# An RMSNorm and QKV projection with Strassen products: four instead of eleven row tiles transposed by TensorE, and a new order of the opening part

## The chip, the cores and the metric

The kernel runs on one core of a Trainium2 chip. A core has five engines that run side by side, each through its own queue in order: TensorE (PE in the profile; its weight loads are PEld), VectorE (DVE), ScalarE (ACT), GpSimd (POOL) and SyncE (SP), which here issues nearly all DMA transfers. Sixteen DMA engines, shared by all transfers, move data between HBM and the core's memory SBUF. TensorE writes only to PSUM, whose eight banks DVE and ACT read out. The metric is the time of one execution on the device in microseconds (us); lower is better.

## What is computed

```python
def reference(x, gamma, w_qkv, eps):      # x: 8 x 1024 x 768, w_qkv: 768 x 2304, float32
    rms = np.sqrt(np.mean(x ** 2, axis=-1, keepdims=True) + eps)
    x_norm = x / rms * gamma
    return np.matmul(x_norm, w_qkv).astype(np.float32)
```

The 8192 rows of x are normalised by their root mean square, scaled by gamma, and multiplied by the weights: an 8192 x 768 by 768 x 2304 product.

## The kernel before

**Tiles.** The rows make 64 tiles of 128. Tiles 0 to 3 are multiplied in bf16 in the plain way (`mm`, L519) while the weights arrive. The other sixty tiles make thirty pairs, 2 to 31, and each pair is multiplied by Strassen's scheme in Winograd's form: the pair's two tiles and the two halves of the 768 inputs give four blocks a11 to a22, the weights of one of three column chunks (768 columns each) give b11 to b22, and seven products of blocks take the place of eight. A product (`product`, L689) is three matmuls of 384 columns in f16.

**Weights.** Sixteen pieces are loaded (`load_w`, L445), multiplied by gamma and cast to bf16 into `w_b` (`conv`: DVE L451, ACT L453, POOL L455). For each chunk an upper bound of the weights is found (`bound` and what follows it) and the quarters are scaled to f16 (`quad`, L617 to L621), and four sums of them are made (`tsum`, L627).

**Rows.** For the first four tiles: `load_x` (L440), `cast` to bf16 and `cp` (both of them L459 on DVE, L461 on ACT), `stat` (L470 and L472: sum of squares and root, ACT), `tr` (transposes by TensorE, L483). For a tile of a pair: `load_x`, `pstat` (L637, ACT), `prms` (L641, ACT), `precip` (L646, DVE), `pcast` to f16 with the row's scale (L651, DVE). Then the tile must be turned so that the inputs lie along the partitions. There are two ways. `ptr` lets TensorE make six transposes into PSUM (L674), and `pcp` copies the result to SBUF (again L459 or L461). `pxbar` is one DMA transpose from SBUF to SBUF, issued by SP (L655). Four sums of the pair's blocks follow (`osum`, L669, DVE or POOL): s1 is read by product 5, s2 by 6, s3 by 7, s4 by 3.

**Results.** The products of a chunk gather in three PSUM banks, and are read out by `hold` (L696 DVE, L698 ACT), `join` (L714, DVE: bank times scale plus a held part) and `last` (L718, ACT). `evac` (L535, L537) does this for the first four tiles. `store` (L541) and `pstore` (L743) are issued by SP. From pair 4 on some results are kept in `w_b`, whose weights are no longer needed then, in areas handed out by `result` in a circle. The last product of all is cut in two (`end_piece`, L725).

**Order.** No scheduler arranges the work: every engine takes its instructions in the order in which the program issues them, and that order is written out. `PLAN` lists the steps of the opening part (everything up to and including pair 14) with a time in us that only sorts them. From pair 15 (`STEADY`) a loop sets the same pattern for each pair and chunk, in slots (0.4875 us, `SLOT`, one product) after `HEAD_END`. Steps of both are merged by their times. In the opening part the plan chooses, step by step, which engine does a conversion, a sum, a hold or a copy, and whether a tile is turned by `ptr` or by `pxbar`. In the regular part all tiles take `pxbar` and all sums are POOL's. Each pair of the loop is prepared ahead:

```python
when((-45, -57)[odd] + 4.5 * i, pcast, t)
when((-42, -54)[odd] + 4.5 * i, pxbar, t)
```

**The start.** PE first turns gamma (`gamma_in`, L552), then runs `idle` (L558), matmuls of zeros that nobody reads, 512 columns each, and then the transposes of the first tiles.

Of the kernel before, what the change touches and what calls it, by code (L numbers as in the profile page):

```python
# [15 lines left out]
HEAD_END = 169.75  # L16
# [3 lines left out]
    (0.000, "load_x", 1), (1.160, "load_x", 3), (4.040, "stat", 1), (4.041, "cast", 1, "DVE"), (4.042, "load_x", 2),  # L20
    (4.043, "gamma_in"), (4.044, "idle", 6, 512), (5.030, "cast", 3, "DVE"), (5.031, "load_w", 2), (5.260, "tr", 1),
    (5.820, "cp", 1, "DVE"), (5.821, "stat", 3), (6.820, "stat", 2), (6.821, "load_w", 3), (6.822, "load_x", 0),
    (6.823, "tr", 3), (6.824, "load_w", 4), (7.480, "conv", 2, 3, "POOL"), (7.481, "load_w", 1),
    (7.482, "cast", 2, "DVE"), (7.483, "tr", 2), (8.141, "conv", 3, 4, "ACT"), (8.142, "cp", 2, "DVE"),
    (8.320, "mm", 1, 0, "3"), (8.660, "mm", 2, 0, "3"), (8.921, "mm", 1, 0, "4"), (9.131, "stat", 0),
    (10.331, "cp", 3, "ACT"), (10.332, "mm", 2, 0, "4"), (10.333, "conv", 4, 5, "POOL"), (10.334, "cast", 0, "DVE"),
    (10.335, "tr", 0), (10.631, "mm", 2, 0, "5"), (10.847, "mm", 1, 0, "5"), (10.848, "load_w", 0),
    (10.849, "cp", 0, "DVE"), (11.062, "mm", 0, 0, "5"), (11.772, "conv", 0, 0, "ACT"),
    (11.773, "conv", 1, 2, "POOL"), (11.774, "mm", 0, 0, "4"), (11.775, "conv", 0, 1, "POOL"), (11.776, "recip", 1),
    (11.777, "mm", 1, 0, "2"), (11.778, "load_w", 6), (11.779, "recip", 2), (11.780, "mm", 0, 0, "2"),  # L30
    (13.092, "conv", 6, 3, "ACT"), (13.093, "conv", 6, 2, "POOL"), (13.094, "load_w", 7),
    (13.095, "mm", 3, 0, "012345"), (13.907, "mm", 2, 0, "012"), (13.908, "recip", 3), (13.909, "recip", 0),
    (13.910, "bound", 0, 1, "DVE"), (13.911, "load_w", 5), (14.107, "evac", 3, 0, "ACT"),
    (14.754, "evac", 2, 0, "ACT"), (14.755, "load_w", 9), (14.756, "load_w", 10), (14.757, "mm", 0, 0, "01"),
    (14.758, "bound", 0, 0, "DVE"), (14.759, "conv", 7, 4, "POOL"), (14.986, "mm", 1, 0, "01"),
    (14.987, "conv", 7, 5, "DVE"), (15.418, "mm", 1, 512, "23"), (15.849, "mm", 0, 512, "23"),
    (15.850, "conv", 5, 0, "DVE"), (16.281, "mm", 0, 512, "54"), (16.282, "conv", 5, 1, "ACT"),
    (16.514, "bound", 1, 0, "DVE"), (16.515, "bound", 0, 2, "ACT"), (16.713, "mm", 2, 512, "23"), (18.254, "fold", 0),
    (18.255, "mm", 1, 512, "01"), (18.256, "mm", 1, 512, "45"), (18.375, "conv", 10, 5, "ACT"), (18.376, "load_w", 8),
    (18.377, "mm", 3, 512, "45"), (18.378, "load_x", 4), (18.544, "bound_tr", 0), (18.664, "mm", 0, 512, "01"),  # L40
    (18.665, "load_x", 5), (19.015, "evac", 1, 512, "ACT"), (19.016, "load_w", 14), (19.017, "conv", 9, 3, "POOL"),
    (19.018, "load_w", 15), (19.019, "conv", 9, 2, "POOL"), (19.615, "evac", 0, 512, "ACT"), (19.616, "bound_top", 0),
    (19.617, "bound_all", 0), (19.618, "mm", 0, 0, "3"), (19.619, "conv", 10, 4, "POOL"),
    (19.695, "conv", 8, 1, "POOL"), (19.696, "scales", 0), (19.697, "mm", 3, 512, "23"),
    (20.375, "quad", 0, "b12", "POOL"), (20.376, "mm", 1, 1024, "23"), (21.645, "quad", 0, "b11", "POOL"),
    (21.646, "mm", 3, 512, "01"), (21.647, "mm", 2, 512, "01"), (21.648, "mm", 1, 1024, "45"),
    (21.649, "conv", 8, 0, "ACT"), (21.650, "pstat", 4), (21.825, "pstat", 5), (21.826, "bound", 1, 2, "DVE"),
    (21.827, "mm", 2, 1024, "45"), (22.150, "mm", 0, 1024, "01"), (22.581, "mm", 2, 512, "45"),
    (23.013, "mm", 1, 1024, "01"), (23.014, "conv", 14, 1, "ACT"), (23.225, "prms", 2),
    (23.226, "bound", 1, 1, "DVE"), (23.227, "evac", 3, 512, "DVE"), (23.228, "load_w", 12), (23.884, "fold", 1),  # L50
    (23.885, "evac", 0, 0, "ACT"), (24.034, "precip", 2), (24.035, "load_w", 13), (24.036, "mm", 2, 1024, "01"),
    (24.075, "conv", 14, 0, "ACT"), (24.076, "mm", 0, 1024, "45"), (24.308, "mm", 2, 1024, "23"),
    (24.309, "tsum", 0, "t1", "DVE"), (24.740, "bound_tr", 1), (24.741, "load_x", 7), (25.060, "bound_top", 1),
    (25.061, "mm", 0, 1024, "23"), (25.062, "conv", 14, 2, "ACT"), (25.063, "quad", 0, "b21", "POOL"),
    (25.291, "mm", 3, 1024, "45"), (25.292, "evac", 2, 512, "ACT"), (25.723, "bound_all", 1),
    (25.843, "mm", 1, 2048, "012"), (25.844, "pcast", 5), (26.171, "mm", 2, 2048, "012"),
    (26.172, "conv", 15, 4, "POOL"), (26.173, "load_x", 6), (26.498, "mm", 3, 1024, "23"),
    (26.499, "evac", 1, 1024, "ACT"), (26.500, "conv", 12, 3, "ACT"), (26.501, "load_x", 17),
    (26.502, "evac", 0, 1024, "DVE"), (26.503, "conv", 15, 5, "POOL"), (26.504, "conv", 12, 2, "POOL"),
    (26.505, "load_w", 11), (26.930, "mm", 3, 2048, "012"), (27.257, "ptr", 5), (27.617, "mm", 3, 1024, "01"),  # L60
    (27.618, "load_x", 9), (27.619, "conv", 15, 3, "POOL"), (27.620, "evac", 2, 1024, "DVE"),
    (27.621, "evac", 1, 0, "DVE"), (28.049, "mm", 3, 2048, "345"), (28.050, "quad", 0, "b22", "ACT"),
    (28.051, "pstat", 7), (28.052, "scales", 1), (28.377, "mm", 0, 2048, "345"), (28.378, "pcp", 5, "DVE"),
    (28.704, "mm", 1, 2048, "345"), (28.945, "evac", 3, 2048, "ACT"), (28.946, "conv", 13, 4, "POOL"),
    (29.475, "store", 3, 2, 2048, 256), (29.476, "conv", 13, 5, "POOL"), (29.477, "pstat", 6),
    (29.478, "mm", 0, 2048, "012"), (29.479, "bound", 2, 1, "DVE"), (30.305, "evac", 0, 2048, "ACT"),
    (30.306, "mm", 2, 2048, "345"), (30.307, "mm", 0, 1536, "45"), (30.695, "prms", 3),
# [295 lines left out]
CW = 384  # L363
# [8 lines left out]
def kernel(  # L372
# [14 lines left out]
    add = mybir.AluOpType.add  # L387
# [6 lines left out]
    Kw, N = w_qkv.shape  # L394
# [297 lines left out]
    def hold(p, c, bank, name, eng):  # L692
# [4 lines left out]
        else:  # L697
            nc.scalar.activation(out=o, in_=pb, func=AF.Copy, scale=SC[c], bias=0.0)  # L698

    spare = []  # L700

    def result(p, c, i, j):
        t = 2 * p + i
# [135 lines left out]
```

## Time and profile before

| what | value |
|---|---|
| median of three runs | 355.81 us (354.83 to 356.18) |
| the profiled execution, whole | 355.04 us |
| its span, first to last instruction | 353.0 us |
| DMA engines' share, 40 to 100 us | 1.03 to 1.07 |
| last weight piece landed | 32.0 us |
| first product of pair 15 | 176.2 us |
| last matmul ends | 349.0 us |

The profile page gives the busy time of each engine, its share of the span, and the number of instructions. The chain of waits starts at the last instruction and goes back, at each step, to what released it: time on that chain is what sets the end. A timeline lists the instructions of one engine in order, equal neighbours merged, with the idle time before each and what ended it. The busy time of PE adds overlapping instructions of a pipeline, so a mean duration there is longer than the time between two starts: product matmuls last 326 ns each and follow one another every 163 ns. The DMA share is packet time over the time of all sixteen engines; packets overlap, so it can pass 1.

### The profile page before, as it was taken

Reading aid. Unit: us, or ns where it says so; the run is one execution under the profiler, and the core shown is the slowest. Engines: PE = TensorE matmul, PEld = TensorE weight load, DVE = VectorE, ACT = ScalarE, POOL = GpSimd, SP = SyncE. Lnnn points to the kernel's source line nnn. Section 1 sums busy time; section 2 is a strip of 40 time slices with the busy share of each in tenths; the row PEclk is TensorE's granted clock in tenths of the full one; section 3 lists DMA queues with packets and bytes.
Section 4 is the critical chain, followed back from the end, with each engine's and each line's share of the span. In section 5 each row is a group of like instructions: output and inputs, shape, how many; then the busy total and the mean of one; then the engine's idle time right before and its main releaser. Section 6 shows DMA issues by size and latency. Waiting matters only on the chain.

```text
span 353.0 us, 6601 instructions
## 1 busy us (share of the span) xinstructions
PE 342.4 (97%) x2113; PEld 203.6 (58%) x2116; DVE 267.1 (76%) x503; ACT 242.6 (69%) x497; POOL 123.5 (35%) x137
## 2 busy tenths in 40 slices
PE   5899999999999999999999999999999999999995
PEld 3346566655666566556556566566566566666653
DVE  3789998988898787676877778676777867676663
ACT  6799898884766665767657576776757676665543
POOL 1496656421041304444354160614407061434000
PEclk9999999999999999999999999999999999999999
DMA  7999999999999899999999999999999999967565
GB/s 275 392 381 351 336 398 364 358 390 377 297 395 331 320 300 318 388 262 382 350 351 355 311 356 320 375 335 334 381 308 332 348 358 353 358 248 277 203 257 223
DMA packets 80637, 117.80 MB, mean 334 GB/s; under 512 B 43606, under 2 KB 45532, under 8 KB 80604
## 3 DMA queue, kind: packets, MB, share of 16 engines
q1 hardware_dynamic: 80448, 117.30, 98.9%
q8 instruction: 16, 0.26, 0.3%
q14 instruction: 17, 0.14, 0.1%
q10 hardware_dynamic: 156, 0.10, 0.1%
HBM read 32.25 MB, written 75.50 MB: 305 GB/s over the span
## 4 chain that ended last, share of the span: by engine, by line
PE 91%; DVE 3%; DMA 2%; SPq 1%; issue 1%; ACT 0%
PE pm L689 84%; PE pm L519 6%; DMA wq<-in_w_qkv_dram 2%; DVE wq L627 1%; PE pm L674 1%; DVE ot L714 1%; DVE xb L651 1%; SPq L445 1%; SPq L440 0%; DVE xT L459 0%; ACT w_b L453 0%; PE pm L725 0%; DVE w_b L714 0%; DVE su L669 0%; ACT pp L698 0%
## 5 line engine op out<-in xcount | busy, mean ns | idle before, releaser
L689 PE MATMUL pm<-wq,su 128*128 128x384 f16 x1080 | 205.6, 326 | 0.4 <-DVE ot L714 0.4
L698 ACT ACTIVATE pp<-pm,sc 128x384 f32<-128x384 f32 x204 | 113.9, 579 | 71.1 <-PE pm L689 70.0
L689 PE MATMUL pm<-wq,xT 128*128 128x384 f16 x807 | 160.9, 326 | 0.6 <-DVE ot L714 0.6
L689 PEld LDWEIGHTS <-su 128*128 128x128 f16 x1080 | 105.3, 98 | 70.4 <-issue 1.2
L714 DVE SCALAR_TENSOR_TENSOR ot<-pm,sc,pp 128x384 f32<-128x384 f32 x172 | 100.2, 612 | 27.0 <-PE pm L689 24.3
L689 PEld LDWEIGHTS <-xT 128*128 128x128 f16 x807 | 78.8, 98 | 52.8 <-issue 1.0
L669 POOL TENSOR_TENSOR su<-xT 128x384 f16<-128x384 f16 x50 | 46.1, 938 | 147.0 <-PE pm L689 71.0
L714 DVE SCALAR_TENSOR_TENSOR w_b<-pm,sc,pp 128x384 f32<-128x384 f32 x98 | 58.4, 615 | 23.6 <-PE pm L689 22.4
L696 DVE TENSOR_SCALAR pp<-pm,sc 128x384 f32<-128x384 f32 x66 | 40.3, 614 | 21.1 <-PE pm L689 20.8
L637 ACT ACTIVATE sq<-x_t 128x768 bf16<-128x768 f32 x60 | 50.2, 836 | 0.7 <-DMA x_t<-in_x_dram 0.4
L651 DVE TENSOR_SCALAR xb<-x_t,rstd 128x768 f16<-128x768 f32 x60 | 39.8, 665 | 0.4
L718 ACT ACTIVATE ot<-pm,sc 128x384 f32<-128x384 f32 x48 | 27.4, 576 | 12.2 <-PE pm L689 11.0
L669 POOL TENSOR_TENSOR su<-xT,su 128x384 f16<-128x384 f16 x28 | 26.2, 936 | 23.1 <-PE pm L689 14.7
L718 ACT ACTIVATE w_b<-pm,sc 128x384 f32<-128x384 f32 x41 | 23.5, 576 | 13.7 <-PE pm L689 13.5
L669 POOL TENSOR_TENSOR su<-su,xT 128x384 f16<-128x384 f16 x26 | 24.9, 958 | 14.3 <-PE pm L689 10.0
L519 PE MATMUL pm<-w_b,xT 128*128 128x512 bf16 (+1 forms) x117 | 25.2, 357 | 1.6 <-POOL w_b L455 0.9
L519 PEld LDWEIGHTS <-xT 128*128 128x128 bf16 x120 | 11.2, 98 | 11.7 <-issue 1.6
L455 POOL TENSOR_SCALAR w_b<-wq,g_sb 128x512 bf16<-128x512 f32 (+1 forms) x16 | 11.6, 731 | 12.6 <-DMA wq<-in_w_qkv_dram 12.6
L637 ACT ACTIVATION_READ_ACCUMULATOR sq<-x_t 128x1 f32 x60 | 11.5, 192 | 0.0
L576 DVE TENSOR_REDUCE bnd<-w_b 128x1 f32<-128x1536 bf16 x6 | 10.3, 1748 | 0.6 <-ACT w_b L453 0.3
L621 POOL TENSOR_SCALAR wq<-w_b,inv 128x1152 f16<-128x1152 bf16 x8 | 9.7, 1224 | 1.8 <-DVE inv L605 1.8
L453 ACT ACTIVATE w_b<-wq,g_sb 128x512 bf16<-128x512 f32 (+1 forms) x12 | 7.8, 666 | 3.3 <-DMA wq<-in_w_qkv_dram 3.1
(56 smaller groups left out, 101.0 us busy)
## 6 DMA issues: line engine op xcount, KB each, us to landing
out_dram<-ot SPq DMA_DIRECT2D x110, 384.0 KB, 4.3
out_dram<-w_b SPq DMA_DIRECT2D x68, 384.0 KB, 4.5
x_t<-in_x_dram SPq DMA_DIRECT2D x64, 384.0 KB, 5.3
wq<-in_w_qkv_dram SPq DMA_DIRECT2D x10, 512.0 KB, 9.3
out_dram<-ot SPq DMA_DIRECT2D x8, 512.0 KB, 6.2
wq<-in_w_qkv_dram SPq DMA_DIRECT2D x4, 256.0 KB, 5.8
xT<-xb SPq DMA_TRANSPOSE x49, 5.0
wq<-in_w_qkv_dram SPq DMA_DIRECT2D x2, 384.0 KB, 9.7
```

The costliest lines, as they stand in the source:

```text
L455: nc.gpsimd.tensor_scalar(out=o, in0=i, scalar1=g, scalar2=1.0, op0=mult, op1=mult)
L519: nc.tensor.matmul(out=PM[t, n0][:, :nl], lhsT=XT[t][:, ko, :], rhs=w_b[:, ko, n0:n0 + nl], start=(b == 1), stop=(b == KO))
L576: nc.vector.tensor_reduce(out=o, in_=v, axis=mybir.AxisListType.XY, op=amax, apply_absolute_value=True)
L621: nc.gpsimd.tensor_scalar(out=o, in0=quad_view(c, q), scalar1=INV[c], scalar2=1.0, op0=mult, op1=mult)
L637: nc.scalar.activation(out=sq, in_=X[t], func=AF.Square, accum_out=SS[p][:, t % 2:t % 2 + 1])
L651: nc.vector.tensor_scalar(out=XB[t], in0=X[t], scalar1=SS[t // 2][:, t % 2:t % 2 + 1], scalar2=None, op0=mult)
L669: (nc.vector if eng == "DVE" else nc.gpsimd).tensor_tensor(out=block(p, q), in0=block(p, x), in1=block(p, y), op=op)
L689: nc.tensor.matmul(out=PB[k][:, :CW], lhsT=block(p, a)[:, ko, :], rhs=WQ[c, b][:, ko, :], start=(first and ko == 0), stop=(ko == KO // 2 - ...
L696: nc.vector.tensor_scalar(out=o, in0=pb, scalar1=SC[c], scalar2=None, op0=mult)
L698: nc.scalar.activation(out=o, in_=pb, func=AF.Copy, scale=SC[c], bias=0.0)
L714: nc.vector.scalar_tensor_tensor(out=result(p, c, i, j), in0=PB[p, c, bank][:, :CW], scalar=SC[c], in1=PART[p, c, held], op0=mult, op1=add)
L718: nc.scalar.activation(out=result(p, c, 1, 0), in_=PB[p, c, "a"][:, :CW], func=AF.Copy, scale=SC[c], bias=0.0)
```

## The change

Seven tiles of the opening part, 6, 8, 11, 13, 15, 17 and 19, are turned by `pxbar` instead of `ptr` and `pcp`; tiles 4, 5, 7 and 9 stay with TensorE, and tile 7's copy goes to ACT, tile 9's to DVE. The whole `PLAN` is written anew: the same loads, products and stores in another order up to pair 14, and other engines for some steps (DVE makes ten conversions instead of two and 20 sums instead of 16; POOL 13 conversions instead of 16 and 32 sums instead of 36; ACT seven conversions instead of twelve and 88 holds instead of 85). At the start tile x0 comes before x3 and weight piece 4 before the others, ACT casts tile 1 and copies tiles 0, 1, 2, and there are 14 fillers instead of six. `HEAD_END` is 3.5 smaller. In the loop the casts and DMA transposes of a pair come 2.8 to 3.8 slots later and 4.1 instead of 4.5 slots apart, and the sums half a slot later; s3 is now made last. The areas of `w_b` for results are taken from a list to which each goes back when its whole store is issued.

```diff
@@ -13,348 +13,345 @@
           6, 1024, 512), (0, 2, 1536, 512), (2, 4, 1536, 512), (4, 6, 1536, 512), (0, 3, 2048,
           256), (3, 6, 2048, 256)]
 
-HEAD_END = 169.75
+HEAD_END = 166.25
 STEADY = 15
 
 PLAN = [
-    (0.000, "load_x", 1), (1.160, "load_x", 3), (4.040, "stat", 1), (4.041, "cast", 1, "DVE"), (4.042, "load_x", 2),
-    (4.043, "gamma_in"), (4.044, "idle", 6, 512), (5.030, "cast", 3, "DVE"), (5.031, "load_w", 2), (5.260, "tr", 1),
-    (5.820, "cp", 1, "DVE"), (5.821, "stat", 3), (6.820, "stat", 2), (6.821, "load_w", 3), (6.822, "load_x", 0),
-    (6.823, "tr", 3), (6.824, "load_w", 4), (7.480, "conv", 2, 3, "POOL"), (7.481, "load_w", 1),
-    (7.482, "cast", 2, "DVE"), (7.483, "tr", 2), (8.141, "conv", 3, 4, "ACT"), (8.142, "cp", 2, "DVE"),
-    (8.320, "mm", 1, 0, "3"), (8.660, "mm", 2, 0, "3"), (8.921, "mm", 1, 0, "4"), (9.131, "stat", 0),
-    (10.331, "cp", 3, "ACT"), (10.332, "mm", 2, 0, "4"), (10.333, "conv", 4, 5, "POOL"), (10.334, "cast", 0, "DVE"),
-    (10.335, "tr", 0), (10.631, "mm", 2, 0, "5"), (10.847, "mm", 1, 0, "5"), (10.848, "load_w", 0),
-    (10.849, "cp", 0, "DVE"), (11.062, "mm", 0, 0, "5"), (11.772, "conv", 0, 0, "ACT"),
-    (11.773, "conv", 1, 2, "POOL"), (11.774, "mm", 0, 0, "4"), (11.775, "conv", 0, 1, "POOL"), (11.776, "recip", 1),
-    (11.777, "mm", 1, 0, "2"), (11.778, "load_w", 6), (11.779, "recip", 2), (11.780, "mm", 0, 0, "2"),
...
-    (32.278, "pcast", 6), (32.725, "quad", 1, "b21", "DVE"), (32.726, "store", 1, 0, 0, 1024),
...
-    (33.500, "product", 2, 0, 5), (33.988, "ptr", 6), (33.989, "pcp", 4, "DVE"), (34.348, "mm", 3, 1536, "01"),
...
-    (36.185, "osum", 2, "s4", "POOL"), (36.186, "mm", 0, 1536, "01"), (36.745, "pcp", 6, "DVE"),
...
-    (50.501, "product", 3, 2, 1), (51.465, "hold", 3, 2, "a", "p1", "ACT"), (51.965, "prms", 5), (51.966, "ptr", 8),
-    (51.967, "tsum", 2, "t1", "DVE"), (51.968, "tsum", 2, "t2", "POOL"), (51.969, "pcast", 9),
...
+    (0.000, "load_x", 1), (1.160, "load_x", 0), (1.580, "load_x", 2), (5.030, "cast", 0, "DVE"), (5.031, "load_w", 4),
+    (5.032, "load_w", 1), (6.820, "cast", 2, "DVE"), (6.821, "cast", 1, "ACT"), (6.822, "stat", 0),
+    (6.823, "load_w", 2), (6.824, "load_w", 3), (6.825, "gamma_in"), (6.826, "idle", 14, 512), (6.827, "tr", 1),
+    (7.480, "conv", 4, 5, "DVE"), (7.481, "tr", 0), (7.482, "cp", 0, "ACT"), (7.483, "tr", 2),
+    (7.484, "cp", 1, "ACT"), (8.050, "mm", 0, 0, "5"), (8.141, "conv", 1, 2, "DVE"), (8.266, "mm", 1, 0, "5"),
+    (8.267, "load_x", 3), (8.801, "conv", 2, 3, "DVE"), (8.802, "cp", 2, "ACT"), (8.803, "mm", 0, 0, "2"),
+    (8.926, "mm", 1, 0, "2"), (9.142, "mm", 2, 0, "5"), (9.371, "mm", 2, 0, "3"), (9.372, "stat", 1),
+    (9.461, "conv", 3, 4, "DVE"), (9.587, "mm", 0, 0, "3"), (9.803, "mm", 1, 0, "3"), (10.031, "mm", 0, 0, "4"),
+    (10.032, "recip", 0), (10.451, "stat", 3), (10.452, "load_w", 0), (11.772, "conv", 0, 1, "POOL"),
+    (11.773, "mm", 2, 0, "4"), (11.774, "conv", 0, 0, "ACT"), (11.775, "cast", 3, "DVE"), (11.776, "mm", 1, 0, "4"),
+    (11.777, "tr", 3), (12.612, "mm", 1, 0, "01"), (13.043, "mm", 0, 0, "01"), (13.044, "load_w", 6),
+    (13.045, "load_w", 7), (13.046, "stat", 2), (13.047, "load_w", 5), (13.092, "conv", 6, 2, "POOL"),
...
+    (32.575, "prms", 3), (32.576, "product", 2, 0, 1), (32.978, "evac", 2, 1024, "DVE"), (32.979, "product", 2, 0, 2),
+    (33.033, "mm", 2, 1536, "45"), (33.034, "hold", 2, 0, "a", "p1", "ACT"), (33.638, "precip", 3),
+    (33.639, "store", 0, 2, 2048, 256), (33.738, "join", 2, 0, 0, 0, "b", "p1"), (34.288, "pcast", 6),
+    (34.289, "load_x", 17), (34.290, "load_x", 16), (34.291, "load_x", 11), (34.998, "osum", 2, "s2", "DVE"),
+    (34.999, "mm", 0, 1536, "23"), (35.000, "mm", 1, 1536, "01"), (35.001, "mm", 2, 1536, "01"),
+    (35.002, "bound", 2, 2, "ACT"), (35.003, "mm", 0, 1536, "01"), (35.191, "mm", 1, 1536, "23"),
+    (35.192, "bound", 2, 0, "ACT"), (35.193, "quad", 1, "b22", "POOL"), (35.623, "product", 2, 0, 5),
+    (35.624, "tsum", 0, "t2", "DVE"), (36.110, "mm", 0, 1536, "45"), (36.111, "pcast", 7),
+    (36.568, "osum", 2, "s4", "DVE"), (36.569, "product", 2, 1, 1), (36.570, "pxbar", 6),
...
+    (47.425, "product", 2, 1, 4), (47.913, "product", 3, 0, 3), (47.914, "store", 2, 0, 0, 1024),
+    (47.915, "store", 0, 0, 0, 1024), (47.916, "join", 3, 1, 1, 1, "a", "p5"), (47.917, "pcast", 8),
+    (47.918, "pstore", 2, 0, 1), (48.478, "pxbar", 8), (49.728, "load_x", 13), (49.729, "product", 3, 1, 4),
...
@@ -654,7 +651,7 @@
         XT[t] = xTp.tile([P, KO, P], f16, name="xT")
         nc.sync.dma_start_transpose(out=XT[t], in_=XB[t])
 
-    SUMS = {"s1": ("a21", "a22", add), "s3": ("a11", "a21", sub), "s2": ("s1", "a11", sub), "s4": ("a12", "s2", sub)}
+    SUMS = {"s1": ("a21", "a22", add), "s2": ("s1", "a11", sub), "s4": ("a12", "s2", sub), "s3": ("a11", "a21", sub)}
 
     def block(p, q):
         if q[0] == "s":
@@ -697,14 +694,14 @@
         else:
             nc.scalar.activation(out=o, in_=pb, func=AF.Copy, scale=SC[c], bias=0.0)
 
-    spare = []
+    spare = [2 * CW * i for i in range(KO * N // (4 * CW))]
+    lent = {}
 
     def result(p, c, i, j):
         t = 2 * p + i
         if (t, "s", c) not in OUT:
             if p >= 4 and (c == 2 or (c == 1 and i == 1 and p % 2 == 0)):
-                s = 2 * CW * (len(spare) % (KO * N // (4 * CW)))
-                spare.append((t, c))
+                s = lent[t, c] = spare.pop(0)
                 OUT[t, "s", c] = w_b.rearrange("p k n -> p (k n)").bitcast(f32)[:, s:s + 2 * CW]
             else:
                 OUT[t, "s", c] = outp.tile([P, 1024], f32, name="ot")
@@ -741,6 +738,8 @@
         j0, j1 = (half[0], half[0] + 1) if half else (0, 2)
         n0 = 2 * CW * c
         nc.sync.dma_start(out=of[t * P:(t + 1) * P, n0 + CW * j0:n0 + CW * j1], in_=OUT[t, "s", c][:, CW * j0:CW * j1])
+        if (t, c) in lent and not half:
+            spare.append(lent.pop((t, c)))
 
 
     N_CH = N // (2 * CW)
@@ -766,12 +765,12 @@
                     t = 2 * p + i
                     when((-96, -103)[odd] + 7 * i, load_x, t)
                     when((-64, -71)[odd] + 7 * i, pstat, t)
-                    when((-45, -57)[odd] + 4.5 * i, pcast, t)
-                    when((-42, -54)[odd] + 4.5 * i, pxbar, t)
+                    when((-41.2, -53.8)[odd] + 4.1 * i, pcast, t)
+                    when((-38.2, -50.8)[odd] + 4.1 * i, pxbar, t)
                 when((-54.5, -61.5)[odd], prms, p)
-                when((-46, -58)[odd], precip, p)
+                when((-42, -54.6)[odd], precip, p)
                 for i, q in enumerate(SUMS):
-                    when(-7 + 0.01 * i, osum, p, q, "POOL")
+                    when(-6.5 + 0.01 * i, osum, p, q, "POOL")
             end = p == MT // 2 - 1 and c == N_CH - 1
             for i, u in ((1, 0), (5, 1), (2, 7.5 if end else 2), (6, 4), (3, 5), (7, 7 if end else 10), (4, 13)):
                 if not (end and i == 4):
```

## The prediction

> **What bounds the kernel now.** I read the page's first two parts, then the PE timeline, the chain of waits, and the timelines of ACT and DVE at the start.
>
> ```profile
> span 353.0 us, 6601 instructions
> ...
> PE 342.4 (97%) x2113; PEld 203.6 (58%) x2116; DVE 267.1 (76%) x503; ACT 242.6 (69%) x497; POOL 123.5 (35%) x137
> ...
> PE 91%; DVE 3%; DMA 2%; SPq 1%; issue 1%; ACT 0%
> ...
> 179.74 167.88 PE pm L689 x1032
> ```
>
> PE is the bound: from 179.74 us to 347.62 us the chain is 1032 product matmuls with no gap, 0.163 us each. The regular part can therefore gain nothing unless PE gets less work; what can change lies before 180 us. Pricing every PE instruction at its pace there (product 3 x 0.163 = 0.488; 512-column matmul 0.216; six f16 transposes 0.34), the work that waits after the first weight block is 333.1 us. That block's matmuls start at 12.89 and the last matmul ends at 349.0, so 3.0 us are lost to waits in between: about 0.6 up to 26 us, 0.1 at 33, 0.7 at 42 to 44, 0.4 at 58 to 73, 0.3 at 155, 0.6 at 180, 0.4 before the end pieces (3.1 with rounding). The other 4.0 us of the span are the last eviction and store, which stay.
>
> ```profile
> 2.77 2.74 PE L558 MATMUL pm<-const-float32-0.0 128*128 128x512 bf16 x6
> 5.31 1.49 PE L483 MATMUL pm<-ident,xb 128*128 128x128 bf16 x12
> 7.27 0.82 PE L483 MATMUL pm<-ident,xb 128*128 128x128 bf16 x6 [0.48 <-DVE xb L459]
> ...
> 10.89 1.46 PE L519 MATMUL pm<-w_b,xT 128*128 128x512 bf16 x6 [0.36 <-POOL w_b L455]
> 12.89 5.99 PE L519 MATMUL pm<-w_b,xT 128*128 128x512 bf16 x26 [0.54 <-ACT w_b L453]
> ```
>
> Columns: start, length, instruction; in brackets the idle time before it and its releaser. The six fillers take 0.43 us each and the first transposes 0.12; later 512-column matmuls take 0.216 and transposes 0.056. The array thus runs at half pace until about 8 us. At 12.89 PE waits for `conv 0,0`, ACT's conversion of the first weight block (DMA landing at 12.09, then 0.73 us).
>
> **Seven tiles leave TensorE.** The plan's transposes by TensorE go from eleven tiles to four (4, 5, 7, 9); tiles 6, 8, 11, 13, 15, 17, 19 take the DMA. PE loses 7 x 6 transposes.
>
> ```profile
> 51.69 0.34 PE pm L674 x6
> ...
> L674 PE MATMUL pm<-ident_h,xb 128*128 128x128 f16 x66 | 5.5, 219 | 0.0
> ...
> L459 DVE COPY xT<-pm 128x768 f16<-128x768 f16 x8 | 4.3, 550 | 0.4 <-PE pm L674 0.3
> ```
>
> The six stand in the chain of waits with 0.34 us (the 219 ns of the group overlap), so PE gains 7 x 0.34 = **-2.4 us**. With them go, net, five DVE copies of 0.55 us and two ACT copies of 0.80 us. DVE also gives up a bound (1.75), three holds (0.61 each), a cast and two copies of the first tiles (0.56 each), and takes eight conversions (0.49 each at full width), four sums (0.35) and an eviction (0.74): some 2 us less before the regular part, in a stretch where it is 88 to 92% busy (40 to 80 us).
>
> What is added is seven DMA transposes, each on SP and on the 16 DMA engines.
>
> ```profile
> xT<-xb SPq DMA_TRANSPOSE x49, 5.0
> ...
> DMA packets 80637, 117.80 MB, mean 334 GB/s; under 512 B 43606, under 2 KB 45532, under 8 KB 80604
> ```
>
> On SP one takes a median of 1.57 us to issue against 0.33 to 0.4 for a plain one, so 11 us more of SP; its issues fill 34 of the 64 us from 36 to 100, so there is room, though stores and loads behind each transpose go 1.5 us later. The DMA engines are the tight place: from 40 to 100 us their share is 1.03 to 1.07. The trace's DMA records show 768 packets of 256 B per transpose, 27 ns on average and 18 at best. That is 768 x 27 / 16 = 1.28 us of all engines, 9.0 us for seven; at 18 ns, 6.0. Loads and stores at their unqueued 122 ns per 3 KB packet leave only 2.4 us idle in those 60 us. Here a rule speaks against the change: the Trainium skill, "DMA: Bandwidth & Descriptors", under Latency and other measured facts, gives a DMA transpose an effective 261 GB/s, hence 0.75 us per 192 KB tile and 5.3 us for seven; its Specifications ask for 512 B and more per transfer for full rate, twice these packets. By the row 6.6 us would find no room, by the rule 2.9; either exceeds the idle time. But full DMA engines are not yet a late PE: PE already ran gapless from 78.20 to 154.60 beside a share of 1.07, except for one transpose of 0.34 us, since stores have buffers. What must arrive in time is the transpose. From issue to landing it takes 2.8 to 6.2 us, median 5.0; the new plan leaves 4 us for tile 8 (transpose at 48.5, first product at 52.5 in its times) and 5 to 6 for tiles 11, 12 and 13. I take 0 for this at PE, with 0 to +3.6 for the range and more for the rival below.
>
> **The start.** The new plan loads x tiles 1, 0, 2 and weights 4, 1, 2, 3 before x tile 3, gives most first conversions to DVE (0.49 us against 0.69 on POOL and 0.72 on ACT), and puts 14 fillers instead of 6 ahead of the transposes. PE takes them in order. From 2.77 us, at 0.43 us each until the pace doubles, and 0.216 after. By the row, half pace to 8.0, 12.2 fillers are done by then and the last at 8.4. The skill's rule ("TensorE: Matmul & The Clock Gate", Part 1) lets the clock rise after one busy window of about 3.4 us, which runs freely against the kernel: between 6.1 and past 8.8, so the fillers end between 7.5 and 8.75, which makes the sum of this part +0.6 to +1.9 where the row gives +1.5. I keep the row's 8.4.
>
> From there the chain runs over ACT, which now copies tiles 0, 1, 2. Two tiles' transposes 0.7 and hand-over 0.15 put the first copy at 9.25; three copies at 0.75 end at 11.5; then `stat 1` and `stat 3`, which the plan sets ahead of `conv 0,0`, cost 1.17 us each (4.00 to 5.17 in ACT's timeline): 13.84; `conv 0,0` at 0.72 ends at 14.56. PE, which has done eleven matmuls before it instead of ten, runs out at about 13.3 and waits. So the dense run starts at **14.6 instead of 12.89: +1.7**, less one matmul of 0.2 done early, **+1.5**. Bounds: a clock at 6.1 us gives 13.7 (+0.6); were the fillers hidden altogether, the block's landing would decide, as now (-0.2); all cold gives 14.95 (+1.9). Behind ACT stand `stat 2`, a bound, and evictions, all later by the same, and the PSUM banks they free.
>
> **The waits behind.** PE is 1.5 us later against DVE and the loads at 15 to 45 us, and DVE has less to do. The wait at 42 is DVE's: the chain stands on DVE from 36.13 to 42.34. I count the waits at 33 and 42 to 44 (0.8) and 0.3 of those at 58 to 73 as hidden: **-1.1**, between 0 (all come back behind the later ACT) and -2.0 (those at 73, 155 and 180 mostly go too).
>
> **At nothing.** The regular part's casts move by 2.8 to 3.8 slots, its sums by half a slot, and s3 goes last, as product 7 (its only reader) is. In the window from 180 us on, 26 casts take 610 to 621 ns and the sums 903 to 922, so they don't hinder one another now; and PE is gapless. If that cover went, a cast ahead of a join would cost PE up to the 0.6 us seen at 180, once. The list of borrowed output areas in `w_b` frees an area when its store is issued instead of taking them in a circle: a join could wait for a store of 4.5 us, hidden by the rest of the list.
>
> **Sum.** -2.4 + 1.5 - 1.1 = **-2.0 us**: span 351.0, that execution 353.0 instead of 355.04. The median before stands 0.77 above it, so I forecast **353.8**.
>
> **Rivals.**
> (1) *The start costs nothing*: the fillers end early or the ACT chain is shorter, and the dense run begins at 12.9. Then -1.7 more: **352.1**. For it: the block lands at 12.1 all the same. Against: ACT's strict order. 24%.
> (2) *The start costs in full and the later waits come back*, as ACT carries its lateness along: -2.4 + 1.5 = -0.9, **354.9**. For it: ACT is 94 to 99% busy from 20 to 40 us, so it doesn't catch up. 16%.
> (3) *The transposes land late*: between 36 and 100 us the DMA engines get 6.0 to 9.0 us more and have 2.4 to spare, and PE waits for the sums of pairs 3 to 9 by the remainder, 3.6 to 6.6 us: 357.4 to 360.4, at the middle **358.9**. It outweighs the gain from 2.0 us on, and shows as slower from 3.8, about 0.55 us for each of the seven tiles. For it: landing takes 5.0 us in the median where the plan leaves 4 to 6. Against: stores can be put off. 10%.
>
> The forecast keeps 50%; its own range is 352.7 to 355.0. A change of 0.5% is 1.8 us, about what a measurement of this kernel can tell from none: faster means under 354.0. Of the forecast's 50, 36 lie there; with rival 1 that is 60. Rival 2, the forecast's other 14 and 2 of rival 3 make 32 within; 8 are left for slower. For 8 in 10 I go from rival 1 less half a microsecond to the forecast plus half of what the returning waits and the cheaper transposes cost together ((1.1 + 3.6) / 2): 351.6 to 356.2.
>
> **What would show it.** Right: 24 transposes under L674; fillers ending near 8.4; `conv 0,0` on ACT ending near 14.5 and PE idle about 1.2 us before it; no DVE wait of PE at 42; the regular part still at 0.163 us. Wrong: PE or the sums waiting for DMA xT<-xb between 40 and 100 us (rival 3), or the dense run starting by 13 (rival 1).

## The result and the profile after

The changed kernel takes **353.52 us** in the median (353.44 to 353.78, four executions) against 355.81 before: a ratio of 0.9941, 95% interval 0.9921 to 0.9962. The forecast was 353.8. The gain is in the medians more than in the two profiled executions: the one of before was 0.77 us below its median and the one of the changed kernel 0.26 above, so whole executions went from 355.04 to 353.78 and spans from 353.0 to 352.0.

The page of the changed kernel, and the last long piece of its chain of waits:

```profile
span 352.0 us, 6558 instructions
...
PE 341.8 (97%) x2079; PEld 201.4 (57%) x2082; DVE 265.3 (75%) x504; ACT 242.1 (69%) x497; POOL 118.0 (34%) x130
...
PE 92%; ACT 4%; DVE 1%; issue 1%; DMA 1%; DVEq 0%; ACTq 0%
...
xT<-xb SPq DMA_TRANSPOSE x56, 5.0
```

```profile
198.63 18.70 PE pm L686 x114
...
219.69 126.96 PE pm L686 x780
```

(Line numbers are three lower than before: the product is L686.) PE is still the bound at 0.163 us a matmul, but the chain is whole only from 219.69 us; before it was whole from 179.74. The start, in PE's timeline:

```profile
2.99 5.65 PE L555 MATMUL pm<-const-float32-0.0 128*128 128x512 bf16 x14
8.48 1.17 PE L480 MATMUL pm<-ident,xb 128*128 128x128 bf16 x18
10.20 0.39 PE L516 MATMUL pm<-w_b,xT 128*128 128x512 bf16 x1 [0.56 <-ACT xT L458]
10.90 2.39 PE L516 MATMUL pm<-w_b,xT 128*128 128x512 bf16 x10 [0.31 <-ACT xT L458]
13.12 0.50 PE L480 MATMUL pm<-ident,xb 128*128 128x128 bf16 x6
14.52 1.67 PE L516 MATMUL pm<-w_b,xT 128*128 128x512 bf16 x6 [0.90 <-ACT w_b L450]
```

The fillers end near 8.5 and the dense run starts at 14.52, behind ACT's `conv 0,0`. ACT's timeline shows why:

```profile
9.35 2.20 ACT L458 COPY xT<-pm 128x768 bf16<-128x768 bf16 x3 [3.23 <-PE pm L480]
11.42 0.87 ACT L467 ACTIVATE sq<-x_t 128x768 bf16<-128x768 f32 x1
...
13.77 0.70 ACT L450 ACTIVATE w_b<-wq,g_sb 128x512 bf16<-128x512 f32 x1
```

Three copies, two `stat` and the conversion, end to end. Behind the start PE loses 2.8 us in all (its timeline against the price of its instructions, as before): 0.5 at 42, 0.1 at 55, 0.4 each at 155 and 199, 0.6 at 220, 0.4 before the end pieces, the rest in small pieces. The one at 42 is new in kind. First before, then the changed kernel's PE, and what its weight loads waited for between 38 and 44 us (us in all, times, longest):

```profile
42.38 0.22 PE L588 MATMUL pm<-ident,bmax 128*1 128x128 bf16 x1 [0.45 <-DVE ot L714]
```

```profile
41.85 1.15 PE L686 MATMUL pm<-wq,xT 128*128 128x384 f16 x6 [0.37 <-ACT pp L695]
```

```profile
PEld L686 <- DMA xT<-xb: 0.8, 1, 0.8
```

Product 3,1,1 reads tile 6, whose DMA transpose landed at 41.81. The timeline names ACT, but the weight load of the same product names the transpose, and PE starts 0.04 us after it landed.

### The profile page after: what moved, and what is told of

Its sections match the earlier page's. It is cut to its first block, busy times and chain, and to the rows that moved or that the text cites. A ratio compares the mean times of both kernels' runs of the same rounds, so it can differ in the third digit from the quotient of the medians.

```text
span 352.0 us, 6558 instructions
## 1 busy us (share of the span) xinstructions
PE 341.8 (97%) x2079; PEld 201.4 (57%) x2082; DVE 265.3 (75%) x504; ACT 242.1 (69%) x497; POOL 118.0 (34%) x130
## 4 chain that ended last, share of the span: by engine, by line
PE 92%; ACT 4%; DVE 1%; issue 1%; DMA 1%; DVEq 0%; ACTq 0%
PE pm L686 85%; PE pm L516 5%; PE pm L555 2%; ACT sq L576 1%; ACT xT L458 1%; DVE ot L711 1%; DMA g<-in_gamma_dram 1%; ACT ot L534 0%; ACT sq L467 0%; ACT pp L695 0%; PE pm L671 0%; DVE xb L648 0%; ACT w_b L450 0%; PE pm L480 0%; DVE pp L693 0%
## 5 line engine op out<-in xcount | busy, mean ns | idle before, releaser
L686 PE MATMUL pm<-wq,su 128*128 128x384 f16 x1080 | 203.8, 326 | 0.3 <-DVE pp L693 0.3
L695 ACT ACTIVATE pp<-pm,sc 128x384 f32<-128x384 f32 x207 | 116.5, 581 | 75.0 <-PE pm L686 72.7
L686 PE MATMUL pm<-wq,xT 128*128 128x384 f16 x807 | 159.3, 326 | 1.0 <-DVE ot L711 0.6
L686 PEld LDWEIGHTS <-su 128*128 128x128 f16 x1080 | 105.5, 98 | 70.1 <-issue 0.5
L686 PEld LDWEIGHTS <-xT 128*128 128x128 f16 x807 | 78.7, 98 | 54.1 <-issue 1.1
L666 POOL TENSOR_TENSOR su<-xT 128x384 f16<-128x384 f16 x52 | 49.6, 956 | 154.3 <-DMA xT<-xb 82.5
L693 DVE TENSOR_SCALAR pp<-pm,sc 128x384 f32<-128x384 f32 x63 | 38.4, 614 | 19.1 <-PE pm L686 18.8
L666 POOL TENSOR_TENSOR su<-su,xT 128x384 f16<-128x384 f16 x24 | 22.7, 948 | 19.6 <-DVE su L666 9.5
L666 POOL TENSOR_TENSOR su<-xT,su 128x384 f16<-128x384 f16 x24 | 22.4, 933 | 8.7 <-DVE su L666 7.0
L452 POOL TENSOR_SCALAR w_b<-wq,g_sb 128x512 bf16<-128x512 f32 (+1 forms) x13 | 8.5, 665 | 18.0 <-DMA wq<-in_w_qkv_dram 18.0
L638 ACT ACTIVATE rms<-ssq,eps_sb 128x2 f32<-128x2 f32 x30 | 8.8, 293 | 0.0
L573 DVE TENSOR_REDUCE bnd<-w_b 128x1 f32<-128x1536 bf16 x5 | 8.6, 1742 | 0.1
(57 smaller groups left out, 94.9 us busy)
```

Source lines behind the costliest of these rows:

```text
L573: nc.vector.tensor_reduce(out=o, in_=v, axis=mybir.AxisListType.XY, op=amax, apply_absolute_value=True)
L638: nc.scalar.activation(out=r, in_=SS[p], func=AF.Sqrt, scale=inv_k, bias=eps_sb)
L666: (nc.vector if eng == "DVE" else nc.gpsimd).tensor_tensor(out=block(p, q), in0=block(p, x), in1=block(p, y), op=op)
L686: nc.tensor.matmul(out=PB[k][:, :CW], lhsT=block(p, a)[:, ko, :], rhs=WQ[c, b][:, ko, :], start=(first and ko == 0), stop=(ko == KO // 2 - ...
L693: nc.vector.tensor_scalar(out=o, in0=pb, scalar1=SC[c], scalar2=None, op0=mult)
```

## The experiments

Each ran beside the kernel before, whose median was 355.22, 355.25 and 355.49 us in the three sets. The last column is (ratio - 0.9940) x 355.4, where 0.9940 is the mean of the two ratios of the changed kernel; each is uncertain by 0.6 to 1.1 us. The second set (three loads behind tile 6, transposes doubled, casts on ACT) was not run with the changed kernel beside it, so there the comparison goes through the kernel before alone.

| kernel | median (range), us | ratio [95%] | against the changed kernel |
|---|---|---|---|
| changed | 353.52 (353.44 to 353.78) | 0.9941 [0.9921, 0.9962] | |
| changed, again | 353.78 (353.02 to 354.28) | 0.9938 [0.9917, 0.9959] | |
| old times of the regular part | 353.95 (351.89 to 354.39) | 0.995 [0.993, 0.997] | +0.4 |
| six fillers | 353.27 (352.99 to 353.83) | 0.9936 [0.9916, 0.9957] | -0.1 |
| `stat 3` behind `conv 0,0` | 354.12 (352.67 to 354.38) | 0.9948 [0.9927, 0.997] | +0.3 |
| seven tiles back to TensorE | 357.49 (356.5 to 358.02) | 1.0054 [1.0035, 1.0073] | +4.1 |
| three loads behind tile 6 | 356.13 (354.93 to 357.35) | 1.0023 [1.0012, 1.0034] | +2.9 |
| the same, six fillers | 355.68 (354.63 to 356.54) | 1.0011 [1.0003, 1.0019] | +2.5 |
| seven transposes made twice | 363.92 (361.87 to 365.09) | 1.024 [1.0212, 1.0268] | +10.7 |
| seven plain copies instead | 356.12 (354.48 to 357.3) | 1.0014 [0.9997, 1.0032] | +2.6 |
| casts on ACT | 356.07 (354.69 to 357.71) | 1.0022 [1.0011, 1.0033] | +2.9 |
| four loads ahead, six fillers | 352.9 (352.38 to 353.88) | 0.9917 [0.9896, 0.9939] | -0.8 |
| the same, tiles 6 and 8 by TensorE | 354.02 (353.48 to 354.42) | 0.9944 [0.9924, 0.9964] | +0.1 |

**The changed kernel again.** 

> The changed kernel once more, unaltered, beside the others of this set. Its four executions lay between 353.44 and 353.78 us; the same is expected, 353.5 within 0.3 us. If it comes out near 355, the differences of 2 us seen in the set before it are of the chip and not of the edits.

It came out at 353.78, so the median repeats. The waits don't repeat in size: here PE's wait for tile 6 is 1.4 us (0.5 in the first execution) and those at 199 and 220 are 0.1 and 0.2. The line of tile 6:

```profile
42.75 1.15 PE L686 MATMUL pm<-wq,xT 128*128 128x384 f16 x6 [1.28 <-DMA xT<-xb]
```

A difference of a microsecond in one wait of one execution is therefore no proof of an edit's effect.

**The new times of the regular part.** The casts, transposes, reciprocals and sums of pairs 15 to 31 go back to their old slots.

```diff
-                    when((-41.2, -53.8)[odd] + 4.1 * i, pcast, t)
-                    when((-38.2, -50.8)[odd] + 4.1 * i, pxbar, t)
+                    when((-45, -57)[odd] + 4.5 * i, pcast, t)
+                    when((-42, -54)[odd] + 4.5 * i, pxbar, t)
...
-                when((-42, -54.6)[odd], precip, p)
+                when((-46, -58)[odd], precip, p)
...
-                    when(-6.5 + 0.01 * i, osum, p, q, "POOL")
+                    when(-7 + 0.01 * i, osum, p, q, "POOL")
```

> Only the regular part's four times are put back (casts at -45/-57, DMA transposes at -42/-54, reciprocals at -46/-58, sums at -7). In the changed kernel's trace three waits of PE in the regular part, 0.43 us at 154.8, 0.38 at 198.6 and 0.62 at 220.2, follow casts of 1.0 to 1.3 us that overlap GpSimd sums. Theory A (the new times put casts beside sums and cost PE): these waits go, casts from 180 us on are back at 0.61 us, and the time falls by 0.7 to 1.4 us against the changed kernel, to about 352.4. Theory B (my step 'at nothing': the times don't matter, the waits come from elsewhere): within 0.4 us of 353.5.

353.95 us: no difference. Waits of PE remain at 156 and 199 us (0.8, 0.3), behind casts of 0.7 to 1.2 us. So the new times neither bring nor cost anything that these runs can tell.

**The start.** First six fillers instead of 14 (`("idle", 6, 512)`), then `stat 3` moved behind `conv 0,0`:

```diff
-    (10.451, "stat", 3),
...
+    (11.7742, "stat", 3),
```

> 6 instead of 14 fillers at the start, nothing else. Theory A (the fillers hold the first transposes back, and with them ACT's chain copy, stat, stat, conv): the dense run of the first weight block starts at 12.9 to 13.3 instead of 14.52, and the time falls by 0.8 to 1.6 us, to 351.9 to 352.7. Theory B (without them the array runs at half pace longer, so the eleven matmuls before the block take 4.7 us instead of 2.4 and end past 13.5): the start moves by less than 0.5 us, the time stays within 0.5 us of 353.5. Theory C (the earlier start is given back at waits for DVE and ACT between 30 and 60 us): start at 12.9 to 13.3, time within 0.5 us.

> On ACT the square sum of tile 3 goes behind the conversion of the first weight block instead of ahead of it; everything else as in the changed kernel. Theory A (ACT's order sets the start): the conversion starts at 12.6 instead of 13.77, PE finishes the matmuls before it at about 13.4 and goes on without a wait, the dense run starts at 13.4, and the time falls by 1.0 us, to 352.5. Theory C (given back at waits for DVE and ACT between 30 and 60 us): start at 13.4, time within 0.4 us of 353.5.

Both starts came earlier, as expected, and both medians stayed. PE's timeline with six fillers, and then with `stat 3` late:

```profile
5.71 2.27 PE L480 MATMUL pm<-ident,xb 128*128 128x128 bf16 x18
8.08 3.09 PE L516 MATMUL pm<-w_b,xT 128*128 128x512 bf16 x11
11.01 0.50 PE L480 MATMUL pm<-ident,xb 128*128 128x128 bf16 x6
12.53 1.67 PE L516 MATMUL pm<-w_b,xT 128*128 128x512 bf16 x7 [1.02 <-ACT w_b L450]
...
49.27 0.65 PE L686 MATMUL pm<-wq,xT 128*128 128x384 f16 x3 [0.56 <-DVE ot L711]
54.87 0.66 PE L686 MATMUL pm<-wq,xT 128*128 128x384 f16 x3 [0.35 <-DMA xT<-xb]
```

```profile
13.32 1.89 PE L1202 MATMUL pm<-w_b,xT 128*128 128x512 bf16 x8
...
42.42 1.15 PE L1372 MATMUL pm<-wq,xT 128*128 128x384 f16 x6 [1.56 <-DMA xT<-xb]
```

With six fillers the dense run starts at 12.53, 2.0 us earlier; PE loses 0.5 us at 40 (tile 6), 0.7 at 49 (a join) and 0.5 at 55 (tile 8), and PE's end comes 0.37 us earlier in these executions. With `stat 3` late PE no longer waits for `conv 0,0`, and the start is 1.2 us earlier; the wait for tile 6 is 1.7 us.

How much of this is the edit shows only over several executions. In eight of the executions here the plan is the changed kernel's up to 30 us, and their dense runs start at 13.04 to 14.52 (middle 13.75); in the four with six fillers it is 12.53 to 13.19 (middle 13.05). So eight fillers less are worth some 0.7 us of the start, not 2.0. With `stat 3` late, 1.2 us stands better: its fillers ended as late as the changed kernel's.

What is saved at the start is waited for behind it. The product that waits for tile 8 starts at 54.9 us in the changed kernel and at 54.9 with six fillers. In five more executions with an unchanged plan up to there it starts at 54.5 to 55.9, and the one whose dense run was earliest (13.04, casts on ACT) lost 2.3 us between 41 and 55 and came to it at 55.3.

**Seven tiles back.** Tiles 6, 8, 11, 13, 15, 17 and 19 return to TensorE, the rest of the new plan unchanged; as for tile 6:

```diff
-    (36.570, "pxbar", 6),
+    (38.070, "ptr", 6), (38.570, "pcp", 6, "DVE"),
```

> Tiles 6, 8, 11, 13, 15, 17 and 19 are transposed by TensorE and copied by DVE again, 1.5 us after the place where the DMA transpose was issued; the rest of the new order stays. Theory A (the gain is the transposes on PE): PE has 7 x 0.34 = 2.4 us more, and the time rises by 2.0 to 3.0 us against the changed kernel, to 355.5 to 356.5. Theory B (the DMA transposes cost PE some of it back as they land late): the rise is only 0.5 to 1.5 us, and waits of GpSimd's sums for DMA xT<-xb before 100 us go. Theory C (DVE, with 7 x 0.55 us of copies more, becomes late): more than 3.5 us.

It is 4.1 us slower. PE's work grows by the 2.4, and PE stands before its own transposes: 1.8 us in three places, of which the two longest are shown. PE's, then DVE's and POOL's timelines of this kernel:

```profile
53.86 0.51 PE L1364 MATMUL pm<-ident_h,xb 128*128 128x128 f16 x6 [1.31 <-DVE xb L1341]
60.72 0.49 PE L1364 MATMUL pm<-ident_h,xb 128*128 128x128 f16 x6 [0.29 <-DVE ot L1404]
```

```profile
51.32 2.48 DVE L1341 TENSOR_SCALAR xb<-x_t,rstd 128x768 f16<-128x768 f32 x1
```

```profile
51.02 2.37 POOL L1317 TENSOR_TENSOR wq<-wq 128x1152 f16<-128x1152 f16 x1 [2.94 <-DVE wq L1317]
```

The cast of tile 9 lies beside POOL's weight sum and takes 2.48 us instead of 0.61; PE, in order, can do nothing else meanwhile. A tile turned by DMA keeps PE out of this. But the places of the seven `ptr` were mine, so the 1.7 us above the 2.4 depend on them: in the kernel before, whose plan was made for these transposes, PE stood 0.0 us before all 66. With the `ptr` so placed, the new order without the seven tiles on DMA is no gain: the ratio is over 1. The converse, the old order with the seven tiles on DMA, was not run, so what the order adds by itself is open.

**Transposes doubled, and copies in their place.** Tiles 10, 11, 12, 13, 15, 17 and 19 are moved a second time, into an area of `w_b` that nobody reads (the list of borrowed areas is one shorter, in both kernels; what that alone costs was not run). Shortened, `unread` standing for that area:

```diff
         nc.sync.dma_start_transpose(out=XT[t], in_=XB[t])
+        if t in (10, 11, 12, 13, 15, 17, 19):
+            nc.sync.dma_start_transpose(out=unread, in_=XB[t])
```

In the second of the two kernels the added line is a plain `nc.sync.dma_start` with the same source and target.

> The changed kernel with seven DMA transposes more: tiles 10, 11, 12, 13, 15, 17 and 19 are transposed a second time, right behind the first, into an area of the weights' buffer that nobody reads; it puts 7 x 192 KB more on the queues and nothing on PE. By the third rival of the prediction (DMA engines 1.03 to 1.07 full between 40 and 100 us, so what is added comes out as PE's waiting) it is 3.6 to 6.6 us slower. By the forecast's step (a late byte is a late store, not a late product) it is within 0.5 us, and PE's waits for DMA xT<-xb between 55 and 100 us stay under 0.5 us in all. In between: each further transpose costs about 0.2 us, 1.5 us in all.

> As the kernel with seven tiles transposed twice, but the second move of each tile is a plain copy of the same 192 KB from SBUF to SBUF, into the same unread area, at the same place of SP's queue. If the DMA engines' time is what is short, seven copies cost what their packets take: 128 packets of 1536 B at some 63 ns (half of the 122 ns of an unqueued 3 KB packet) over 16 engines are 0.5 us each, 3.5 us in all, so 2 to 4 us over the changed kernel where the transposes cost 10.4. If it is the transfer as such (a place in SP's queue, a completion that others wait for), it is as slow as with the transposes, 9 us or more over it. If only the transposing is dear and plain bytes find room, under 1 us.

Seven further transposes cost **10.7 us**, seven copies of the same bytes **2.6**. With the transposes PE waits in places where it did not before (of the four waits for DMA, one of 0.7 us is the old one at tile 6). The table of PE's waits (engine, line, releaser: us in all, times, longest):

```profile
PE pm L693 <- DMA xT<-xb: 5.4, 4, 1.9
...
PE pm L693 <- ACT pp L702: 2.1, 1, 2.1
PE pm L693 <- DVE ot L718: 1.5, 2, 1.0
```

The 2.1 of ACT goes back along the chain of waits to an x load of 7.29 us, landing at 178.7. Behind it PE ran slow for a while. Its timeline, and the window (length, then the busy time of PE, PEld, DVE, ACT and POOL with the number of instructions, then the granted clock, DMA share and GB/s):

```profile
181.15 2.12 PE L693 MATMUL pm<-wq,xT 128*128 128x384 f16 x6
```

```profile
180.00:182.00 2.00, 1.76 (x6) 0.84 (x6) 1.78 (x4) 1.31 (x4) 0.00 (x0) 0.56 1.12 373
```

Eleven matmuls start 0.32 us apart instead of 0.163, at a granted clock of 0.56. That is 1.7 us of this execution's loss; 6.6 us of waiting lie between 75 and 108 us, and 2.3 before 180.2. The third rival's mechanism is thus real, and dearer than I made it. In the windows from 60 to 110 us, first the changed kernel, then this one:

```profile
60.00:110.00 50.00, 50.00 (x309) 30.13 (x308) 42.35 (x86) 36.25 (x79) 13.00 (x14) 1.00 1.08 325
```

```profile
60.00:110.00 50.00, 44.30 (x267) 25.42 (x265) 37.38 (x75) 31.40 (x69) 11.92 (x12) 1.00 1.06 289
```

The share is full in both; the rate falls from 325 to 289 GB/s, as is expected where transposes take 1.28 us of all engines for 192 KB. SP's issues were dense there too (1.2 to 2.5 us for each transpose, 0.5 to 0.65 for a copy), so how the 8 us between transposes and copies divide between the DMA engines and SP's queue stays open.

**Three loads behind tile 6.** The loads of x tiles 17, 16 and 11 go behind its transpose on SP, with 14 and with six fillers.

```diff
-    (34.289, "load_x", 17), (34.290, "load_x", 16), (34.291, "load_x", 11),
...
     (36.570, "pxbar", 6),
+    (36.5701, "load_x", 17), (36.5702, "load_x", 16), (36.5703, "load_x", 11),
```

> The changed kernel with one thing altered: on SP the three loads of x tiles 17, 16 and 11 are issued behind the DMA transpose of tile 6 instead of just ahead of it. Theory C (the opening part is tied to the landing of the transposes of tiles 6 and 8, so work ahead of them is given back there): tile 6 lands some 2 us earlier, near 39.5 us, the 0.7 us wait of PE at 42 us goes, and the time falls by 0.5 to 0.9 us unless tile 8 takes it over at 55 us (its wait grows from 0.26). Rival (PE meets other late work there: DVE's sums or the PSUM banks): the wait at 42 us stays within 0.2 us and the time too, within 0.3 us of the changed kernel.

> The changed kernel with six fillers instead of 14, and the loads of x tiles 17, 16 and 11 behind tile 6's DMA transpose on SP. Theory C: the dense run starts some 2 us earlier, as with six fillers alone, but now the wait for tile 6 (0.68 us there) is gone or under 0.3 us, so PE is some 1 us ahead of the changed kernel at 45 us; tile 8's landing near 54.9 us takes back a part, and the end is 0.5 to 1.5 us earlier than the changed kernel's. Rival (the DMA engines are full, so each byte sent later comes late elsewhere): the gain over the changed kernel stays under 0.5 us, and PE waits for x tiles' statistics or for tile 8 by 1 us or more.

The wait at 42 went, as the theory said, and yet the kernel lost 2.9 us (2.5 with six fillers, whose earlier start brought no more than 0.4). The windows around it, the changed kernel and then this one:

```profile
36.00:42.00 6.00, 5.63 (x36) 2.99 (x34) 5.96 (x13) 5.91 (x11) 0.05 (x1) 1.00 1.05 291
```

```profile
36.00:42.00 6.00, 6.00 (x40) 3.46 (x38) 5.95 (x13) 5.91 (x11) 0.82 (x1) 1.00 0.64 169
42.00:60.00 18.00, 15.00 (x92) 8.21 (x90) 13.31 (x29) 13.30 (x28) 7.28 (x6) 1.00 1.01 346
```

SP stood before the transpose until 36.43 us, when the cast was done, with nothing queued ahead of it, and the DMA engines ran dry. The bytes came later, in two ways that reach PE. ACT, in its order, stood before the sum of squares of tile 9, whose load was behind the three, and the hold behind it came late (1.4 us of PE at 47.8). The stores came later too, and DVE had no free buffer for a result (1.5 us of PE at 52.3). ACT's and DVE's timelines of this kernel:

```profile
46.32 0.84 ACT L1320 ACTIVATE sq<-x_t 128x768 bf16<-128x768 f32 x1 [2.28 <-DMA x_t<-in_x_dram]
```

```profile
50.27 0.62 DVE L1397 SCALAR_TENSOR_TENSOR ot<-pm,sc,pp 128x384 f32<-128x384 f32 x1 [3.70 <-DMA out_dram<-ot]
51.58 0.62 DVE L1397 SCALAR_TENSOR_TENSOR ot<-pm,sc,pp 128x384 f32<-128x384 f32 x1 [0.69 <-DMA out_dram<-ot]
```

So tile 6 was not the tie but a sign of it. My theory of a single late transpose falls. What fits these runs in its place: up to some 60 us **the DMA engines bound the opening part, and what they stand idle there is paid at the end**. This run shows it for a hole that was made; whether filling one gains is the next question.

**Four loads ahead.** The theory says where to gain: in the changed kernel SP waits 7.0 us, until 31.30, before the first store of a result, with loads behind it. The loads of x tiles 8, 17, 16 and 11 are moved ahead of that store (their old places, at 30.238 and 34.289 to 34.291, go); six fillers.

```diff
-    (6.826, "idle", 14, 512),
+    (6.826, "idle", 6, 512),
...
     (29.574, "load_x", 12),
+    (29.5741, "load_x", 8), (29.5742, "load_x", 17), (29.5743, "load_x", 16), (29.5744, "load_x", 11),
     (29.575, "pstat", 7), (29.818, "store", 3, 2, 2048, 256),
```

> The changed kernel with six fillers, and the loads of x tiles 8, 17, 16 and 11 ahead of the first store of a result on SP, which waits for its eviction until 29 to 31 us while the DMA engines run empty (share 0.60 to 0.83 between 30 and 36 us in the changed kernel). Theory E (the DMA engines bind the opening part; what they stand idle there is lost, and 1.6 us of idle time lie between 30 and 36 us): the share there rises to 1.0, the wait for tile 6 near 40 us falls under 0.3 us, and the end is 0.7 to 1.6 us before that of the six fillers alone, near 352.2 us. Rival (PE's own order binds it: waits for DVE, ACT and PSUM banks): within 0.3 us of the six fillers alone, 353.3.

> As the kernel with six fillers and the four loads ahead, and tiles 6 and 8 turned by TensorE again (six transposes and a copy by DVE each, 1.5 us behind the place of their DMA transposes). Theory E: the DMA engines get back 2 x 1.4 us, SP no longer stands before the two transposes until the casts are done, and PE pays 2 x 0.34 us: 0.3 to 1.5 us faster than with the four loads ahead alone, near 351.5. Rival (as when all seven were put back: PE meets its own transposes before the casts and the copies are done): 0.7 us or more slower than that.

With the loads ahead the median is **352.9 us**, the lowest of all; but against the six fillers alone the ratio falls by 0.0019 (0.7 us) and the intervals overlap, so the gain is not shown beyond the noise. From 30 to 36 us, the changed kernel and then this one:

```profile
30.00:36.00 6.00, 5.95 (x42) 3.79 (x42) 5.74 (x13) 5.33 (x10) 5.65 (x6) 1.00 0.73 232
```

```profile
30.00:36.00 6.00, 5.87 (x31) 2.96 (x31) 5.58 (x9) 5.68 (x11) 5.63 (x6) 1.00 1.03 392
```

The hole is filled and the wait for tile 6 gone, at the small end of what was expected: tile 8 still cost 0.5 us at 54.5 and a join 0.5 at 48.9. With tiles 6 and 8 on TensorE as well, the rival looks right: 1.0 us slower than this by the ratios (intervals just overlap), with the same wait of 1.31 us before `ptr 9` for the same cast of 2.48 us.

**Casts on ACT.** In the regular part `pcast` becomes an activation:

```diff
+        if t >= 2 * STEADY:
+            nc.scalar.activation(out=XB[t], in_=X[t], func=AF.Copy, scale=SS[t // 2][:, t % 2:t % 2 + 1], bias=0.0)
+            return
```

> The changed kernel with the regular part's casts (tiles 30 to 63) on ACT instead of DVE. Theory D (the waits of PE at 154.8, 198.6 and 220.2 us, 1.4 us in all, come from a DVE cast that meets GpSimd's sums and takes 1.0 to 1.3 us instead of 0.61, so a join on DVE is late for its PSUM bank): the three waits go, and the end is 0.8 to 1.4 us earlier. Rival (ACT, which holds and reads out banks too, goes from 69% to some 80% busy and is late in its place): the waits stay or grow, and the time is the same or up to 2 us longer.

The rival was right, by more than it said: 2.9 us longer, where it had up to 2. The waits at 154.8, 198.6 and 220.2 went (the last two were nearly gone in the changed kernel's second execution too), and six new ones of 0.5 us came, one for every second pair, 21 us apart. The first, in PE's timeline, and what ACT did before it:

```profile
194.29 1.14 PE L689 MATMUL pm<-wq,su 128*128 128x384 f16 x6 [0.33 <-ACT pp L698]
```

```profile
192.28 0.19 ACT L634 ACTIVATION_READ_ACCUMULATOR sq<-x_t 128x1 f32 x1
192.38 0.57 ACT L718 ACTIVATE w_b<-pm,sc 128x384 f32<-128x384 f32 x1
192.84 0.93 ACT L649 ACTIVATE xb<-x_t,rstd 128x768 f16<-128x768 f32 x1
193.66 0.57 ACT L698 ACTIVATE pp<-pm,sc 128x384 f32<-128x384 f32 x1
```

A hold has to stand behind the cast of 0.93 us, and PE wants the bank 0.3 us before it is read out. That the casts meet POOL's sums on DVE is seen (0.84 to 1.02 us at 151 to 154 us, sums up to 1.22); what it costs PE could not be won back this way.

## Why the prediction came out right, step by step

- **Seven tiles leave TensorE, -2.4.** Right: 24 transposes were left, and putting the seven back costs 2.4 us of PE's work. That putting them back cost 4.1 us in all does not make leaving worth more: the waits before casts and copies came with the places I gave the `ptr`, and in the kernel before PE stood at no transpose of these tiles.
- **The start, +1.5.** Right in place and cause: the dense run stands behind ACT's chain, with 0.90 us of waiting before it. That it starts at 14.52 against the 14.6 worked out is in part luck. "Half pace until about 8 us" was read from one execution; in nine executions with these fillers the pace doubled between 5.4 and 8.1 us, and in the eight with ACT's order unchanged the dense run started at 13.04 to 14.52. The running window that the prediction weighed and set aside (6.1 to past 8.8, so 3.4 us or more after the first filler) comes nearer, though two of the nine, at 2.5 and 3.0 us after it, lie below. As a term of the sum +1.5 was too large: undoing it by the fillers moves the median by 0.1 to 0.3 us. The first rival, which started early and counted all of that, was wrong for that reason.
- **The waits behind, -1.1.** Mis-sized, and the step that failed: 2.8 us are left where 1.9 were expected, so -0.2 instead of -1.1. DVE's wait at 42 went, as said, but tile 6's DMA transpose took its place, and three waits from 155 us on came in. This error and that of the start have opposite signs, and they belong together: a later start hides waits, an earlier one lays them bare.
- **The transposes' landing, 0.** Nearly: 0.5 us at 42 and 0.1 at 55 (1.4 at 42 in the second execution). The reason given holds in the bytes: by 100 us the trace has 31.1 MB of loads and stores (packets over 256 B) in the changed kernel and 34.4 before, by 180 us 57.1 and 58.5, by 300 us 94.9 and 95.3. The stores were put off and caught up. But that cover was almost used up, since the next seven transposes cost their full price. For that price the rule that the prediction weighed (the Trainium skill, "DMA: Bandwidth & Descriptors", under Latency and other measured facts: 261 GB/s, which the row gives for a non-contiguous middle dimension, hence an estimate of 5.3 us for seven) is about half of the 10.7 us measured; the row's 9.0 us is near it, and nearer still without the 1.7 us at the low clock. The third rival failed in the step "2.4 to spare": what can be put off is more than what stands idle. The 2.4 was also counted with two prices. A count of the packets from 40 to 100 us leaves some 2.7 us with the 18 ns that is the median of a transpose packet (not its best, 15), and nothing with the 27 ns put on the new ones.
- **At nothing.** The new times of the regular part are worth nothing, as priced. The ground given, casts of 610 to 621 ns and no gap from 180 us on, held for the execution of before alone: in the changed kernel some casts take 1.0 to 1.3 us from 150 to 235 us, three waits of 0.4 to 0.6 us follow such casts, and with the old times put back the same is seen. The list of borrowed areas was not run alone.
- **The base.** Adding 0.77 for the execution of before was right for this result: -2.0 was foretold, the medians moved by 2.3 (1.7 in the last set). The two profiled executions alone, at -1.3, would have shown a smaller gain. In these two PE's last matmul ends 1.0 us earlier (348.0 after 349.0), where the sum says 2.0: the tiles and the start came as worked out, the waits did not. So the terms were met to a microsecond, and that the medians fall within 0.3 us of the forecast is luck of the size of their scatter.

## What to carry to other kernels

Where PE and the DMA engines are both full, an earlier start can gain nothing unless the transfers come earlier too (two runs here); look for stretches where the DMA share falls below 1 and ask which in-order instruction holds up the queue. A transfer that waits for a computation belongs behind those that wait for nothing: the reverse cost 2.9 us here. A shift of work to DMA is free only as long as something there can be put off, so price it at its full engine time and ask how much can be. And read a start, or a single wait, from more than one execution before a sum is built on it.

## What was not expected of the hardware

- A DMA transpose of 192 KB cost 1.5 us of the kernel's time where no cover was left (10.7 for seven, of which 1.7 at the low clock in the profiled execution), a plain copy of the same bytes 0.4.
- After a wait of PE of 2.15 us at 180 us the granted clock stood at 0.54 for 3.5 us, in one execution of one kernel; after a wait of 1.9 us at 87 us in the same execution it did not fall.
- The same 14 fillers took between 4.4 and 5.8 us in nine executions (four of these kernels' profiles ended them by 7.5 us, the changed kernel's near 8.5): the pace of the matmuls doubled 2.5 to 5.5 us after the first of them. The end hardly followed it, for the reason above.
- A DVE cast beside a weight sum on POOL took 2.48 us instead of 0.61, in two kernels at the same place.
